# Norms of a two-layer decoder step on one core: a third staging tile, the second group's norm steps in front of the splitting of weights, and a last norm with its factors in PSUM

## The chip, the core and the metric

The kernel runs on one core of one Trainium2 chip. The metric is the device time of one execution in microseconds. The profiled execution has a span of 1143.7 us, from its first to its last instruction, and a mean granted TensorE clock of 0.989 (1.00 is 2.4 GHz, a level at half of it is 1.2 GHz).

## What is computed

One inference step of a decoder with two layers, in f32, for 512 new prompt tokens and 8 sample tokens, 1024 features. Each layer has a mixer (attention over a sliding window in the first, gated linear attention, GLA, in the second) and a gated ConvFFN, and behind each of these four sublayers stands a layer norm. The change is in the norms.

```python
def layer_norm(x, g, b):
    mu = jnp.mean(x, -1, keepdims=True)
    var = jnp.mean(jnp.square(x - mu), -1, keepdims=True)
    return (x - mu) * lax.rsqrt(var + LN_EPS) * g + b

for i in range(DEPTH):                                   # DEPTH = 2
    m = swa(x, ...) if i % 2 == 0 else gla(x, ...)       # with w_qkv / w_gla, w_mix_o
    x = layer_norm(ALPHA * x + m, ln_mix_g[i], ln_mix_b[i])
    f = conv_ffn(x, ...)        # gelu(causal_conv3(x @ w_gate)) * (x @ w_value) @ w_down
    x = layer_norm(ALPHA * x + f, ln_ffn_g[i], ln_ffn_b[i])
```

## The kernel before, in words

**Data.** Features lie on the partitions: `x` is 8 tiles of 128 features by the tokens. The 520 tokens form two groups, a (256) and b (264). To keep f32 accuracy each operand of a product is split into a high part and a low part (`wh`, `wl` of a weight; `xh`, `xl` of x; for group a both parts lie in `xs_a`, for b they are `xh_b`, `xl_b`), and a product is three matmuls: `wh`·`xh` (L193), `wh`·`xl` (L195), `wl`·`xh` (L196).

**Units.** A unit is 128 output features of one weight, which for a group takes 8 x 3 matmuls into one PSUM bank `accp`. The units follow each other through the phases: attention's q, k, v (10), its output projection (8), the first FFN (three parts, each of `w_up` units and 8 `w_down` units), GLA, its output projection, and the second FFN. Group a runs 4 or 5 units ahead of b (`LEADS`), so that a's norm can run while b's last products fill TensorE, and b's norm while a's first products of the next phase do.

**Weights.** `load_unit` issues a 512 KB load on SP's queue into a staging tile `raw` (`RAWS` of them, 2), ScalarE copies the high part (`wh`, L165) and VectorE subtracts it for the low part (`wl`, L168). A staging tile is free again when its `wl` is done. There are `WSLOTS` = 6 slots for split weights, and one more pool for an extra unit at the start of an FFN. I call the units of the phase behind a norm e, e+1, and so on. At three of the four norms the weights of e+1 to e+5 are "late": they are split in `parts` (L177, L179), held by `issue_after` behind instructions of a's norm. The extra unit is e+6, split at L165 and L168.

**The norm.** `ln_chunk` runs behind each output unit: it adds the product to x (L243 or L245), squares it on ScalarE (L263) and adds to the running sums (L275, L276; most of b's on GpSimd, the last ones on VectorE). `ln_end` multiplies the sums by ones on TensorE (L283 and L285, into the PSUM banks `tp` and `pv`), copies the mean (L288) and its square (L289) on ScalarE, subtracts the mean from six of the eight x tiles on GpSimd (L291) and from two on VectorE (L299), forms minus the variance `nv` (L292), takes its logarithm and an exponential on ScalarE (L300, L301), improves that by one Newton step on VectorE (L302, L303, L305) and has the factor in `pv`. Then for each of the 8 tiles VectorE scales (L321), ScalarE writes the high part (L322) and VectorE the low part (L323). ScalarE's first Gelu of the new phase (L620) needs another table, and TensorE's first matmul of b in the new phase needs `xh_b`.

**The last norm** writes no high and low parts. VectorE scales pairs of tiles (L311), ScalarE (L314) or VectorE (L316) applies gain and bias, and SP stores each pair of y (L317).

**What sets the order.** The program is written unit by unit. Generators that `yield n` are resumed n slots later (`spawn`, `due`), and each engine's final order is chosen by a scheduler at build time from the dependences and its own time line.

Of the kernel before, what the change touches and what calls it, by code (L numbers as in the profile page):

```python
# [95 lines left out]
class Net:  # L96
# [74 lines left out]
    def parts(self, u, h, l, r):  # L171


        norm = self.norm if self.norm and self.slot < self.norm[0] else None
        behind = lambda ins: self.tc.issue_after(ins) if norm else ExitStack()
        with behind(norm and norm[1]):
# [57 lines left out]
    def ln_chunk(self, g, m, ps, scaled, last=False):
# [41 lines left out]
        (nc.gpsimd if m < p2 else nc.vector).tensor_tensor(g.s2, g.s2, q, op=ALU.add)  # L276

    def ln_end(self, g, i, last=False):
# [23 lines left out]
        nc.vector.tensor_tensor(q, r, r, op=ALU.mult)  # L302
        nc.vector.scalar_tensor_tensor(q, q, 0.5, nv, op0=ALU.mult, op1=ALU.mult)  # L303
        rp = r if last else e2
        nc.vector.scalar_tensor_tensor(rp, q, 1.5, r, op0=ALU.add, op1=ALU.mult)  # L305
# [834 lines left out]
```

## Time and profile before

| | |
|---|---|
| median of 3 runs | 1143.75 us (1142.8 to 1144.4) |
| profiled execution | 1145.38 us, span 1143.7 us |
| TensorE (PE) busy | 1105.9 us, 97% of the span, 8806 matmuls |
| VectorE (DVE) busy | 784.1 us, 69% |
| ScalarE (ACT) busy | 566.9 us, 50% |
| GpSimd (POOL) busy | 321.8 us, 28% |
| DMA | 122.81 MB, 107 GB/s over the span |

TensorE is busy for nearly all of the span, so the places to look at are the few in which it is not, and what ended each of these waits. Times within the program are us from the span's start.

### The profile page before, as it was taken

How to read it: one execution, taken by the hardware profiler on the slowest of the kernel's cores; microseconds unless marked ns; L12 is line 12 of the kernel's file. 1: busy time of each engine (PE TensorE's matmuls, PEld its weight loads, DVE VectorE, ACT ScalarE, POOL GpSimd, SP SyncE). 2: the span in 40 equal slices, each digit the busy share in tenths (PEclk: the TensorE clock that was granted, in tenths of full speed). 3: DMA queues.
4: the chain of work that ended last, by engine and by line, in shares of the span. 5: the costliest groups of instructions: out<-in, count | busy, mean ns of one | idle time of the engine just before them, and what ended most of it. 6: DMA issues, size and time to landing. Idle time of an engine off the chain costs nothing.

```text
span 1143.7 us, 22908 instructions
## 1 busy us (share of the span) xinstructions
PE 1105.9 (97%) x8806; PEld 1056.7 (92%) x8806; DVE 784.1 (69%) x1628; ACT 566.9 (50%) x1251; POOL 321.8 (28%) x589
## 2 busy tenths in 40 slices
PE   8999998999999999999899999998999999999995
PEld 7997798999999999999899999898999999999994
DVE  8897578755665566568867877788755665566657
ACT  5677555534553245435545655455524553245433
POOL 4575584400110001255311100383400110011344
PEclk9999999999999999999899999999999999999998
DMA  7453022333323223242125355332333232232222
GB/s 239 150 178 93 16 75 93 111 93 119 103 93 109 94 95 109 75 132 96 56 87 162 114 176 173 118 101 92 111 98 125 93 109 95 93 112 93 75 64 75
DMA packets 53788, 122.81 MB, mean 107 GB/s; under 512 B 6792, under 2 KB 27312, under 8 KB 53680
## 3 DMA queue, kind: packets, MB, share of 16 engines
q1 hardware_dynamic: 51664, 119.61, 32.7%
q10 hardware_dynamic: 2016, 1.75, 0.5%
q8 instruction: 69, 1.13, 0.4%
q14 instruction: 39, 0.32, 0.1%
HBM read 108.67 MB, written 8.47 MB: 102 GB/s over the span
## 4 chain that ended last, share of the span: by engine, by line
PE 74%; DVE 12%; DMA 5%; ACT 3%; issue 2%; POOL 2%; SPq 0%; ACTq 0%; DVEq 0%; POOLq 0%
PE accp L214 15%; PE accp L195 15%; PE accp L193 15%; PE accp L196 15%; PE accp L215 8%; DMA vb<-dv 3%; DVE wl L168 1%; DVE xs_a L323 1%; DVE wl L179 1%; DMA raw<-in_w_up 1%; DVE sgla L877 1%; DMA raw<-in_w_qkv 1%; DVE x_a L321 1%; DMA qs<-hl 1%; PE pv L521 1%
## 5 line engine op out<-in xcount | busy, mean ns | idle before, releaser
L168 DVE TENSOR_TENSOR wl<-raw,wh 128x1024 fp32r<-128x1024 f32 (+2 forms) x174 | 210.5, 1212 | 110.5 <-ACT wh L165 109.9
L165 ACT ACTIVATE wh<-raw 128x1024 fp32r<-128x1024 f32 (+2 forms) x170 | 175.9, 1035 | 208.3 <-PE accp L195 187.2
L193 PE MATMUL accp<-xh_b,wh 128*128 128x264 f32 x976 | 271.7, 278 | 7.4 <-ACT xh_b L322 7.4
L195 PE MATMUL accp<-xl_b,wh 128*128 128x264 f32 x976 | 270.6, 278 | 0.0
L196 PE MATMUL accp<-xh_b,wl 128*128 128x264 f32 x976 | 270.5, 277 | 0.0
L214 PE MATMUL accp<-xs_a,wh 128*128 128x512 f32 x576 | 196.3, 382 | 0.0
L193 PEld LDWEIGHTS accp<-xh_b,wh 128*128 128x128 f32 x976 | 185.0, 190 | 8.3 <-ACT xh_b L322 7.8
L195 PEld LDWEIGHTS accp<-xl_b,wh 128*128 128x128 f32 x976 | 184.6, 189 | 2.5 <-issue 0.4
L196 PEld LDWEIGHTS accp<-xh_b,wl 128*128 128x128 f32 x976 | 184.4, 189 | 0.8 <-issue 0.6
L215 PE MATMUL accp<-xs_a,wl 128*128 128x256 f32 x576 | 145.4, 273 | 0.0
L193 PE MATMUL accp<-hh_b,wh 128*128 128x264 f32 x480 | 134.0, 279 | 1.7 <-ACT hh_b L221 1.2
L195 PE MATMUL accp<-hl_b,wh 128*128 128x264 f32 x480 | 134.4, 280 | 0.3 <-DVE hl_b L561 0.2
L196 PE MATMUL accp<-hh_b,wl 128*128 128x264 f32 x480 | 133.6, 278 | 0.0
L214 PEld LDWEIGHTS accp<-xs_a,wh 128*128 128x128 f32 x576 | 109.1, 189 | 11.4
L193 PE MATMUL accp<-xs_a,wh 128*128 128x256 f32 x400 | 113.6, 286 | 0.9 <-ACT wh L165 0.9
L196 PE MATMUL accp<-xs_a,wl 128*128 128x256 f32 x400 | 112.6, 284 | 1.4 <-DVE wl L168 0.8
L215 PEld LDWEIGHTS accp<-xs_a,wl 128*128 128x128 f32 x576 | 110.2, 191 | 1.9
L195 PE MATMUL accp<-xs_a,wh 128*128 128x256 f32 x384 | 109.0, 284 | 0.6 <-DVE xs_a L222 0.3
L193 PEld LDWEIGHTS accp<-hh_b,wh 128*128 128x128 f32 x480 | 91.5, 191 | 2.4 <-ACT hh_b L221 1.6
L195 PEld LDWEIGHTS accp<-hl_b,wh 128*128 128x128 f32 x480 | 91.3, 190 | 1.8 <-DVE hl_b L561 0.4
L196 PEld LDWEIGHTS accp<-hh_b,wl 128*128 128x128 f32 x480 | 91.4, 190 | 0.2
L225 POOL COPY hist<-aext 128x2 f32<-128x2 f32 x44 | 10.7, 244 | 276.8 <-DVE aext L608 274.0
(327 smaller groups left out, 2500.5 us busy)
## 6 DMA issues: line engine op xcount, KB each, us to landing
raw<-in_w_up SPq DMA_DIRECT2D x88, 512.0 KB, 3.4
raw<-in_w_down SPq DMA_DIRECT2D x32, 512.0 KB, 3.4
raw<-in_w_gla SPq DMA_DIRECT2D x24, 512.0 KB, 3.4
raw<-in_w_mix_o SPq DMA_DIRECT2D x16, 512.0 KB, 4.1
raw<-in_w_down SPq DMA_DIRECT2D x16, 384.0 KB, 3.0
qs<-hl SPq DMA_DIRECT2D x64, 64.0 KB, 2.1
sgla<-in_state_gla SPq DMA_DIRECT2D x16, 256.0 KB, 2.8
vb<-dv SPq DMA_DIRECT2D x16, 256.0 KB, 3.7
```

Source lines behind the costliest of these rows:

```text
L165: nc.scalar.activation(h[:, c], r[:, c], AF.Copy)
L168: nc.vector.tensor_tensor(l[:, c], r[:, c], h[:, c].bitcast(F32), op=ALU.subtract)
L179: self.nc.vector.tensor_tensor(l, r, h.bitcast(F32), op=ALU.subtract)
L193: nc.tensor.matmul(o, h[:, ks], xh, start=k == 0, stop=False)
L195: nc.tensor.matmul(o, h[:, ks], xl, start=False, stop=False)
L196: nc.tensor.matmul(o, l[:, ks], xh, start=False, stop=not tail and k == nt - 1)
L214: both = lambda: nc.tensor.matmul(o, h[:, ks], in_turn(rs[:, k].rearrange("p t q j -> p t (q j)")), start=k == 0, stop=last)
L215: low = lambda: nc.tensor.matmul(o[:, :P], l[:, ks], in_turn(rh[:, k]), start=False, stop=False)
L321: v = nc.vector.scalar_tensor_tensor(x[:, m], x[:, m], sc(m), rp, op0=ALU.mult, op1=ALU.mult)
L323: xl = nc.vector.scalar_tensor_tensor(g.xl[:, m], parted(x[:, m]), bi(m), g.xh[:, m].bitcast(F32), op0=ALU.add, op1=ALU.subtract)
L521: mm = nc.tensor.matmul(pv[64 * v:64 * v + 64, b * P:(b + 1) * P], self.vtok[:, kb, 64 * v:64 * v + 64], parts[v][w][:, b], start=i == 0, ...
L877: late(nc.vector.scalar_tensor_tensor(s[:, j], vb[:, j], kraw[:, b:b + 1], s[:, j], op0=ALU.mult, op1=ALU.add))
```

## The change

Five edits, in the diff below.

- `RAWS` is 3: a load may start when the third last unit's low part is done.
- `parts` takes a place j instead of the norm's state and holds the two splits behind marked instructions: the first late unit (j = 1) behind a's exponential and a's scales, j = 2 behind a's low parts, j = 3 and 4 behind b's sums, and j = 5 (unit e+5) and j = 6 (the extra unit, which is late too now) behind b's exponential and b's factor.
- Group a's 8 scales come first, and its 8 low parts 3 slots later in a piece, behind b's latest addition to x. Group b's low parts come behind all its scales too.
- Two tiles of the norm share others' room (`sb` takes `nv`'s, `sa` takes `r`'s).
- In the last norm `nv`, the Newton step and the factor are in PSUM, VectorE subtracts the mean from four tiles (from PSUM) and GpSimd from four, and each pair's scale is held behind the affine step of VectorE on the pair before, with ScalarE on tiles 0, 1, 2, 4, 6 and VectorE on 3, 5, 7.

```diff
-RAWS = 2
+RAWS = 3
...
             if late:
-                self.spawn(self.parts(u, h[:, c], l[:, c], r[:, c]), 1)
+                self.spawn(self.parts(late, h[:, c], l[:, c], r[:, c]), (0, 1, 2, 2, 2, 1, 0)[late])
...
+    def parts(self, j, h, l, r):
+        for _ in range(3):
+            yield 0
+        behind = lambda what: self.tc.issue_after(self.marks[what]) if what in self.marks else ExitStack()
+        with behind({1: "exp_a", 3: "high_a", 5: "exp_b", 6: "exp_b"}.get(j)):
             self.nc.scalar.activation(h, r, AF.Copy)
-        with behind(norm and norm[2 if u == norm[4] else 3]):
+        with behind({1: "rows_a", 2: "low_a", 3: "sums_b", 4: "sums_b", 5: "factor_b", 6: "factor_b"}[j]):
             self.nc.vector.tensor_tensor(l, r, h.bitcast(F32), op=ALU.subtract)
...
+        if last:
+            nv, vr = self.mtile("sc")[:, :n], self.mtile("sc")[:, :n]
-        for m in range(2, KD) if last else range(NSUB):
+        for m in range(2, NSUB) if last else range(NSUB):
             nc.gpsimd.tensor_tensor(x[:, m], x[:, m], mu, op=ALU.subtract)
...
             if last:
-                nc.vector.tensor_tensor(x[:, 0:2], x[:, 0:2], mu.unsqueeze(1).broadcast_to([P, 2, n]), op=ALU.subtract)
+                for xp in (x[:, 0:2], x[:, NSUB:KD]):
+                    nc.vector.tensor_tensor(xp, xp, e1.unsqueeze(1).broadcast_to([P, 2, n]), op=ALU.subtract)
...
+        if last:
+            nc.vector.tensor_tensor(vr, nv, r, op=ALU.mult)
+            q = nv
+            nc.vector.scalar_tensor_tensor(q, vr, 0.5, r, op0=ALU.mult, op1=ALU.mult)
+        else:
+            nc.vector.tensor_tensor(q, r, r, op=ALU.mult)
+            nc.vector.scalar_tensor_tensor(q, q, 0.5, nv, op0=ALU.mult, op1=ALU.mult)
+        rp = e2
+        factor = nc.vector.scalar_tensor_tensor(rp, q, 1.5, r, op0=ALU.add, op1=ALU.mult)
...
+                with self.tc.issue_after(behind) if behind else ExitStack():
+                    nc.vector.tensor_tensor(xp, xp, rp.unsqueeze(1).broadcast_to([P, 2, n]), op=ALU.mult)
                 for j in (m, m + 1):
-                    if j in (0, 2, 4, 5, 7):
+                    if j in (0, 1, 2, 4, 6):
                         nc.scalar.activation(x[:, j], x[:, j], AF.Identity, scale=sc(j), bias=bi(j))
                     else:
-                        nc.vector.tensor_scalar(x[:, j], x[:, j], sc(j), bi(j), op0=ALU.mult, op1=ALU.add)
+                        behind = nc.vector.tensor_scalar(x[:, j], x[:, j], sc(j), bi(j), op0=ALU.mult, op1=ALU.add).ins
...
         for m in range(KD):
             v = nc.vector.scalar_tensor_tensor(x[:, m], x[:, m], sc(m), rp, op0=ALU.mult, op1=ALU.mult)
+            xh = nc.scalar.activation(g.xh[:, m], parted(x[:, m]), AF.Identity, bias=bi(m))
+        self.marks.update({"rows_" + g.name: v.ins, "high_" + g.name: xh.ins})
         if g.i == 0:
+            yield 3
+            yield 0
+        with ExitStack() if g.i else self.tc.issue_after(self.marks["add_b"]):
+            for m in range(KD):
+                xl = nc.vector.scalar_tensor_tensor(g.xl[:, m], parted(x[:, m]), bi(m), g.xh[:, m].bitcast(F32), op0=ALU.add, op1=ALU.subtract)
...
-            late = not extra and self.units[u][1] and any(e - 5 <= done < e for e in (...))
+            e = min((p for p in self.phases[2:4] + self.phases[5:] if p > u - WSLOTS), default=u)
+            late = late or (0 if extra else max(0, u - e))
```

The first place is VectorE's order in b's first norm (behind attention's output projection), from b's last sums on; line numbers are those of the kernel that each piece is of. Before:

```order
L275 TENSOR_TENSOR s_b<-s_b,x_b 128x264
L276 TENSOR_TENSOR s_b<-s_b,sq 128x264
L610 SCALAR_TENSOR_TENSOR conv<-aext,par,conv 128x256
L611 SCALAR_TENSOR_TENSOR conv<-aext,par,conv 128x256
L179 TENSOR_TENSOR wl<-raw,wh 128x1024 x2
L292 SCALAR_TENSOR_TENSOR nv<-msq,pv 128x264
L299 TENSOR_TENSOR x_b<-x_b,tp 128x264 x2
L610 SCALAR_TENSOR_TENSOR conv<-aext,par,conv 128x256
L302 TENSOR_TENSOR msq<-r 128x264
L611 SCALAR_TENSOR_TENSOR conv<-aext,par,conv 128x256
L632 TENSOR_TENSOR hprod<-conv,accp 128x256
L303 SCALAR_TENSOR_TENSOR msq<-msq,nv 128x264
```

Behind these rows come L168 (`wl` of the extra unit), L632, L305, L222 and the 8 scales L321. And of the change, where L271 and L272 are the sums, L178 is `wl`, L291 is `nv`, L647 multiplies behind the Gelu, L310 forms the factor and L329 scales:

```order
L271 TENSOR_TENSOR s_b<-s_b,x_b 128x264
L272 TENSOR_TENSOR s_b<-s_b,sq 128x264
L178 TENSOR_TENSOR wl<-raw,wh 128x1024 x2
L625 SCALAR_TENSOR_TENSOR conv<-aext,par,conv 128x256
L626 SCALAR_TENSOR_TENSOR conv<-aext,par,conv 128x256
L291 SCALAR_TENSOR_TENSOR nv<-msq,pv 128x264
L299 TENSOR_TENSOR x_b<-x_b,tp 128x264 x2
L307 TENSOR_TENSOR msq<-r 128x264
L647 TENSOR_TENSOR hprod<-conv,accp 128x256
L308 SCALAR_TENSOR_TENSOR msq<-msq,nv 128x264
L310 SCALAR_TENSOR_TENSOR pv<-msq,r 128x264
L178 TENSOR_TENSOR wl<-raw,wh 128x1024
```

The second convolution's two steps, one of the two products with hprod and the extra unit's `wl` (the last row) have gone behind the factor. Next come 5 scales (L329), the `wl` of unit e+5 (before the second of the two ahead of `nv`), and the other 3 scales. The two `wl` ahead of `nv` are those of e+3 and e+4 now, and one `wl` fewer stands ahead of the sums.

The second place is TensorE's order around the first matmul of b in the new phase, with buffer numbers; `wh_2404` is the weight of unit e. Before, `wh_2660` being that of unit e+5:

```order
L193 MATMUL accp_2904<-xs_a_86,wh_2660 128x256
L195 MATMUL accp_2904<-xs_a_86,wh_2660 128x256
L196 MATMUL accp_2904<-xs_a_86,wl_2661 128x256
L193 MATMUL accp_2933<-xh_b_89,wh_2404 128x264
L193 MATMUL accp_2975<-xs_a_86,wh_2737 128x256
L195 MATMUL accp_2975<-xs_a_86,wh_2737 128x256
```

And of the change, where `wh_2658` and `wl_2659` are those of unit e+5:

```order
L194 MATMUL accp_2870<-xs_a_86,wl_2615 128x256
L191 MATMUL accp_2904<-xs_a_86,wh_2658 128x256
L193 MATMUL accp_2904<-xs_a_86,wh_2658 128x256
L191 MATMUL accp_2933<-xh_b_89,wh_2404 128x264
L194 MATMUL accp_2904<-xs_a_86,wl_2659 128x256
L191 MATMUL accp_2904<-xs_a_86,wh_2658 128x256
```

Before, all 24 matmuls of a with e+5 stand in front of b's first matmul; now 2 do, and the 22 others stand behind it, the first of them with `wl_2659`. The norm before the second FFN has the same shape.

The third place is VectorE's end of the program, from b's `nv` on. Before:

```order
L292 SCALAR_TENSOR_TENSOR nv<-msq,pv 128x264
L296 TENSOR_TENSOR x_b<-x_b,mu 128x528
L302 TENSOR_TENSOR msq<-r 128x264
L303 SCALAR_TENSOR_TENSOR msq<-msq,nv 128x264
L305 SCALAR_TENSOR_TENSOR r<-msq,r 128x264
L311 TENSOR_TENSOR x_b<-x_b,r 128x528 x3
L316 TENSOR_SCALAR x_b<-x_b,par 128x264
L311 TENSOR_TENSOR x_b<-x_b,r 128x528
L316 TENSOR_SCALAR x_b<-x_b,par 128x264 x2
```

And of the change, where `tp`, `pv` and `sc` are PSUM banks:

```order
L291 SCALAR_TENSOR_TENSOR sc<-msq,pv 128x264
L296 TENSOR_TENSOR x_b<-x_b,tp 128x528 x2
L303 TENSOR_TENSOR sc<-sc,r 128x264
L305 SCALAR_TENSOR_TENSOR sc<-sc,r 128x264
L310 SCALAR_TENSOR_TENSOR pv<-sc,r 128x264
L320 TENSOR_TENSOR x_b<-x_b,pv 128x528 x2
L325 TENSOR_SCALAR x_b<-x_b,par 128x264
L320 TENSOR_TENSOR x_b<-x_b,pv 128x528
L325 TENSOR_SCALAR x_b<-x_b,par 128x264
L320 TENSOR_TENSOR x_b<-x_b,pv 128x528
L325 TENSOR_SCALAR x_b<-x_b,par 128x264
```

One instruction more subtracts the mean, each of the seven others between it and the affine steps has one operand in PSUM, and the pairs end one after the other.

## Rows read from the trace of the kernel before

**Rows 1.** Windows: stretch and length, busy us (instructions) by engine, clock, DMA share, GB/s

```profile
30.00:140.00 110.00, 104.41 (x930) 94.89 (x929) 88.39 (x269) 73.63 (x263) 65.21 (x119) 0.98 0.38 110
160.00:175.00 15.00, 14.90 (x131) 14.58 (x130) 14.85 (x26) 8.16 (x17) 9.93 (x11) 1.00 0.19 58
175.00:190.00 15.00, 11.22 (x94) 10.90 (x95) 12.74 (x23) 10.05 (x20) 7.71 (x11) 1.00 0.48 154
...
540.00:560.00 20.00, 17.30 (x109) 15.28 (x109) 18.12 (x42) 11.89 (x29) 6.07 (x6) 0.83 0.16 53
```

**Rows 2.** TensorE's waits: what waited and for what, us in total, times, longest

```profile
PE accp L193 <- ACT xh_b L322: 7.4, 2, 3.9
PE accp L704 <- ACT v_a L771: 2.5, 1, 2.5
```

**Rows 3.** Windows behind the waits of b's first and second norm, columns as in rows 1

```profile
188.00:192.00 4.00, 2.80 (x18) 2.80 (x18) 4.00 (x11) 4.00 (x10) 0.18 (x1) 0.79 0.37 131
...
552.00:556.00 4.00, 4.00 (x20) 3.71 (x20) 3.60 (x10) 0.49 (x2) 0.00 (x0) 0.56 0.00 0
```

**Rows 4.** Timeline of DVE, b's first norm: start, us, instruction, count [idle before <-releaser]

```profile
167.30 3.48 DVE L323 SCALAR_TENSOR_TENSOR xs_a<-x_a,par,xs_a 128x256 fp32r<-128x256 f32 x6
...
175.19 0.42 DVE L276 TENSOR_TENSOR s_b<-s_b,sq 128x264 f32<-128x264 f32 x1
...
179.97 1.23 DVE L179 TENSOR_TENSOR wl<-raw,wh 128x1024 fp32r<-128x1024 f32 x1 [1.44 <-ACT wh L177]
181.11 0.42 DVE L292 SCALAR_TENSOR_TENSOR nv<-msq,pv 128x264 f32<-128x264 f32 x1
181.45 0.76 DVE L299 TENSOR_TENSOR x_b<-x_b,tp 128x264 f32<-128x264 f32 x2
...
185.41 1.76 DVE L168 TENSOR_TENSOR wl<-raw,wh 128x1024 fp32r<-128x1024 f32 x1
...
187.43 0.43 DVE L305 SCALAR_TENSOR_TENSOR pv<-msq,r 128x264 f32<-128x264 f32 x1
...
188.10 3.28 DVE L321 SCALAR_TENSOR_TENSOR x_b<-x_b,par,pv 128x264 f32<-128x264 f32 x8
```

**Rows 5.** Timeline of ACT in the same stretch

```profile
178.88 1.06 ACT L177 ACTIVATE wh<-raw 128x1024 fp32r<-128x1024 f32 x1 [1.61 <-DMA raw<-in_w_up]
179.84 0.36 ACT L288 COPY mu<-tp 128x264 f32<-128x264 f32 x1
...
182.46 1.28 ACT L620 ACT_TABLE_LOAD   x1
...
188.62 3.63 ACT L322 ACTIVATE xh_b<-x_b,par 128x264 fp32r<-128x264 f32 x8
```

**Rows 6.** Timeline of POOL, b's first and last norm

```profile
180.28 5.81 POOL L291 TENSOR_TENSOR x_b<-x_b,mu 128x264 f32<-128x264 f32 x6 [3.54 <-ACT mu L288]
...
1130.70 5.74 POOL L291 TENSOR_TENSOR x_b<-x_b,mu 128x264 f32<-128x264 f32 x6 [7.47 <-ACT mu L288]
```

**Rows 7.** Timeline of DVE, b's last norm

```profile
1128.91 0.42 DVE L243 TENSOR_TENSOR x_b<-x_b,accp 128x264 f32<-128x264 f32 x1
...
1132.33 0.57 DVE L302 TENSOR_TENSOR msq<-r 128x264 f32<-128x264 f32 x1 [0.32 <-ACT r L301]
...
1133.82 0.86 DVE L305 SCALAR_TENSOR_TENSOR r<-msq,r 128x264 f32<-128x264 f32 x1
1134.71 2.91 DVE L311 TENSOR_TENSOR x_b<-x_b,r 128x528 f32<-128x528 f32 x3
...
1138.50 0.73 DVE L316 TENSOR_SCALAR x_b<-x_b,par 128x264 f32<-128x264 f32 x2
```

**Rows 8.** Timeline of PE, the last matmul of the last product

```profile
1128.04 0.28 PE L196 MATMUL accp<-hh_b,wl 128*128 128x264 f32 x1
```

**Rows 9.** Timeline of SP's queue, the last stores

```profile
1138.02 2.24 SPq L317 DMA_DIRECT2D out_y<-x_b  x4
```

**Rows 10.** Timeline of PE at the start, TensorE's last wait for a weight there

```profile
24.47 0.38 PE L193 MATMUL accp<-xs_a,wh 128*128 128x256 f32 x1 [0.38 <-ACT wh L165]
```

More of the change, by code (lines that the diff above doesn't have):

```diff
@@ L56 @@
 LATEB = 14
-HOLD = 5
 WIDE = 4
@@ L169, in load_unit @@
         self.w[u] = (h, l)
[L171 to L176, printed above, removed]
+    def parts(self, j, h, l, r):
[3 more added lines that the diff above has]
+        with behind({1: "exp_a", 3: "high_a", 5: "exp_b", 6: "exp_b"}.get(j)):
             self.nc.scalar.activation(h, r, AF.Copy)
-        with behind(norm and norm[2 if u == norm[4] else 3]):
+        with behind({1: "rows_a", 2: "low_a", 3: "sums_b", 4: "sums_b", 5: "factor_b", 6: "factor_b"}[j]):
             self.nc.vector.tensor_tensor(l, r, h.bitcast(F32), op=ALU.subtract)
-        yield from ()
     def product(self, g, u, rh, rl):
@@ L228, in mtile @@
         return self.mps.tile([P, 512], F32, name=tag, bufs=2 if tag == "sc" else 1)
-    def next_phase(self):
-        return min(p for p in self.phases if p > self.unit)
     def ln_chunk(self, g, m, ps, scaled, last=False):
@@ L242, in ln_chunk @@
         if scaled:
-            nc.vector.tensor_tensor(x[:, m], x[:, m], ps, op=ALU.add)
+            add = nc.vector.tensor_tensor(x[:, m], x[:, m], ps, op=ALU.add)
         else:
-            nc.vector.scalar_tensor_tensor(x[:, m], x[:, m], ALPHA, ps, op0=ALU.mult, op1=ALU.add)
+            add = nc.vector.scalar_tensor_tensor(x[:, m], x[:, m], ALPHA, ps, op0=ALU.mult, op1=ALU.add)
+        self.marks["add_" + g.name] = add.ins
         if m == 0:
@@ L253, in ln_chunk @@
             if not scaled:
-                sa = c("sa")
+                sa = c("r")
                 nc.scalar.activation(sa, mp, AF.Copy, scale=KD / ALPHA)
@@ L301, in ln_end @@
         self.exp = nc.scalar.activation(r, r, AF.Exp, scale=-0.5).ins
[L302 to L305, printed above, removed]
+        if last:
[7 more added lines that the diff above has]
+        factor = nc.vector.scalar_tensor_tensor(rp, q, 1.5, r, op0=ALU.add, op1=ALU.mult)
+        self.marks.update({"exp_" + g.name: self.exp, "factor_" + g.name: factor.ins})
         sc = lambda m: self.par[:, C_LNG + i * KD + m:C_LNG + i * KD + m + 1]
@@ L321, in ln_end @@
             v = nc.vector.scalar_tensor_tensor(x[:, m], x[:, m], sc(m), rp, op0=ALU.mult, op1=ALU.mult)
-            nc.scalar.activation(g.xh[:, m], parted(x[:, m]), AF.Identity, bias=bi(m))
-            xl = nc.vector.scalar_tensor_tensor(g.xl[:, m], parted(x[:, m]), bi(m), g.xh[:, m].bitcast(F32), op0=ALU.add, op1=ALU.subtract)
+            xh = nc.scalar.activation(g.xh[:, m], parted(x[:, m]), AF.Identity, bias=bi(m))
+        self.marks.update({"rows_" + g.name: v.ins, "high_" + g.name: xh.ins})
         if g.i == 0:
-            self.norm = self.slot + HOLD, self.exp, v.ins, xl.ins, self.next_phase() + 1
+            yield 3
[3 more added lines that the diff above has]
+                xl = nc.vector.scalar_tensor_tensor(g.xl[:, m], parted(x[:, m]), bi(m), g.xh[:, m].bitcast(F32), op0=ALU.add, op1=ALU.subtract)
+        self.marks["low_" + g.name] = xl.ins
         for m in range(KD):
@@ L982, in more, with next_unit @@
         return self.nu < end - XEND
-    def next_unit(self, extra):
+    def next_unit(self, extra, late=0):
         u = self.nu
@@ L987, in next_unit @@
             self.nu += 1
-            done = u - WSLOTS
-            late = not extra and self.units[u][1] and any(e - 5 <= done < e for e in (*self.phases[2:3], *self.phases[3:4], *self.phases[5:6]))
+            e = min((p for p in self.phases[2:4] + self.phases[5:] if p > u - WSLOTS), default=u)
+            late = late or (0 if extra else max(0, u - e))
             self.load_unit(u, extra=extra, late=late)
@@ L998, in run @@
         self.attn_open()
-        self.later, self.slot, self.seq, self.norm = [], 0, 0, None
+        self.later, self.slot, self.seq, self.marks = [], 0, 0, {}
         for i, u in self.order():
@@ L1002, in run @@
             _, _, f, a, pre = self.units[u]
-            if i == 1:
-                self.unit = u
             if i == 0 and pre:
```

8 lines of the change are left out of this document (4 added, 4 removed).

## The prediction

> **What bounds the kernel now.** I read the windows first. In 160 to 175 us TensorE is busy for 14.90 of 15 us with 131 matmuls, one in 0.114 us, and that is how most of the program looks [rows 1]. A change to the norms can therefore only win where TensorE stands. The windows show three such places outside the two ends: 5.6 us spread over attention (30 to 140), 3.8 us in 175 to 190 and 2.7 us in 540 to 560, there with the clock at 0.83 [rows 1]. The third norm has the shape of the first. Then the waits: TensorE waits twice for `xh_b`, 7.4 us in total, the longer 3.9, at the norms ahead of the two FFNs, and once for 2.5 us at the norm ahead of GLA [rows 2]. That last one is put down to `v_a`, but what the matmul at L704 reads is `xh_b`, which ScalarE writes there after it. Each wait costs more than its length: in the 4 us behind the first the granted clock is 0.79, in 552 to 556 it is 0.56 [rows 3], which is nearly all of that stretch at 1.2 GHz.
>
> Now back from the wait, in the timelines of the first norm. `xh_b` begins at 188.62 [rows 5], just behind the first of the scales at 188.10, which had to wait for the factor (L305) at 187.43, and ahead of that stood a 1.76 us `wl` [rows 4]. The chain begins with `nv` at 181.11. The sums were issued at 175.19, so 5.9 us lie between the sums and `nv`. In them VectorE's `wl` stood 1.44 us for ScalarE's `wh` [rows 4], which itself stood 1.61 us for a load, and ScalarE's copy of the mean was queued behind that `wh` [rows 5]. So a late load delays the norm. This is what the third staging tile and the new order act on.
>
> The end is the other place: the last product's last matmul starts at 1128.04 [rows 8], and the last stores are issued from 1138.02 on for 2.24 us [rows 9]. All 10 us between are the last norm, with nothing beside it.
>
> **First norm of b, step by step.** *Up to `nv`.* One `wl` of about 1.2 us fewer stands ahead of the sums on VectorE, which had no idle time there, so the sums end near 174.4 in place of 175.6. The three tiles let the loads of e+3 and e+4 start one unit sooner, by more than the 1.61 us of the wait, so I cost that wait at nothing now. Then come two `wl` (1.2 each, up to 1.76 beside GpSimd [rows 4]) and two steps of the convolution of some 0.5: `nv` would stand between 177.9 and 179. I take 178.5, 2.6 us earlier, for GpSimd's six subtractions (5.81 us [rows 6]) now begin with the earlier mean and lie beside these `wl`.
>
> *From `nv` to `xh_b`.* Before, ScalarE's table load starts 1.35 us behind `nv` (182.46 [rows 5]) and takes 1.28; the Gelu behind it takes some 0.4. In the new order the product with hprod needs this Gelu and stands ahead of the last two factor steps, so three steps of about 0.4 (as L305 [rows 4]) end at 1.35 + 1.28 + 0.4 + 1.2 = 4.3 behind `nv`. The extra unit's `wl` (1.2), the first scale (3.28/8 = 0.41 [rows 4]) and its high part (3.63/8 = 0.45 [rows 5]) follow: the first `xh_b` is ready 6.35 us behind `nv`, at 184.9. Before it was ready at 189.1. That is 4.2 us gained on this chain.
>
> *What is late next.* TensorE doesn't cash it in. Its order puts b's first matmul 22 matmuls sooner, behind only two of unit e+5, so it arrives 22 x 0.114 = 2.5 us earlier, at about 183. And the next matmul in its queue reads `wl` of e+5, which VectorE does behind the five scales: 4.3 + 1.2 + 5 x 0.41 + 1.2 = 8.75 behind `nv`, 187.3. The whole of a's unit e+5 is queued behind this matmul, and b's next ones behind that. The 22 matmuls that before lay ahead of the wait bring TensorE at 187.3 + 2.5 = 189.8 to where it was at 189.1: +0.7. With `nv` at 177.9 it is +0.1. The 8 low parts of a, in a piece behind b's additions now, make TensorE wait for some of a's tail products (0.58 each [rows 4], as GpSimd works beside them), but this only uses up time that it would stand at 183 anyway. I take +0.3 for this norm and the same for the third. The low clock behind the wait stays.
>
> **Second norm.** There is no Gelu and no table between `nv` and the factor: 1.35 + 3 steps of 0.4 + 1.2 + 0.41 + 0.45, so `xh_b` stands about 4.6 behind a `nv` that comes 2.6 earlier, where in the first norm before it was 8.0. The 2.5 us wait [rows 2] goes. With the clock, (1 - 0.83) x 20 = 3.4 us at stake in this window [rows 1], up to 5.9 us could be won. But VectorE now does b's scales (3.28) and half of b's low parts (4 x 0.41) ahead of the scan of GLA's decay, 4.9 us, and a's q and k and the state's products wait for that. So a second wait, on the decay, takes the place of part of the first. Between 0 and -5.9 I take -2.7, just short of half.
>
> **Last norm.** Factors: L302, L303 and L305 take from 1132.33 to the first pair at 1134.71, 2.4 us, at up to 0.86 each with two SBUF operands beside GpSimd's subtractions [rows 6, 7]. With one operand in PSUM the same shape takes 0.38 to 0.43 though GpSimd works (L299 at 181.45 [rows 4]). The two subtractions of the mean that VectorE now makes take 1.4 and end 0.35 after the exponential, so 2.4 becomes 0.35 + 1.1: -0.9. Pairs: 2.91/3 = 0.97 each, the last affine step ends at 1139.23 [rows 7], 4.5 us behind the first pair's start; now four of about 0.70 and three affine steps of 0.36, then 0.25 of ScalarE's last step: 4.1, -0.4. The mean: b's last addition starts 0.6 behind the last matmul's end [rows 7, 8], because VectorE is busy with a's last norm, which gets shorter by the same means: -0.5. Stores: the four are issued in 2.24 us in a row [rows 9]; spread out, the last finds the queue free: -0.3. Sum -2.1, between 0 (transfers decide) and -3.
>
> The Trainium skill's page "VectorE: DVE Perf Modes", section "Rules for kernel authors", speaks against this part: for elementwise work on a matmul's output it wants either the 1x rate accepted or the data copied from PSUM to SBUF first where many operations follow, and the change goes the other way. By that rule factors and pairs win nothing and the tail would give -0.8, the whole -3.3. The trace differs in this stretch: 0.38 from PSUM against 0.86 from SBUF alone.
>
> **Start and scheduler.** The third tile lets a load of the start begin sooner: TensorE's 0.38 us wait [rows 10] goes, -0.4. What the scheduler shuffles elsewhere, in attention above all, I cost at 0; the cover there is TensorE's queue, and without it no more than the 5.6 us idle in 30 to 140 [rows 1] can be won or half as much lost; I let it count for 1.5 either way.
>
> **Sum.** -0.4 + 0.3 - 2.7 + 0.3 - 2.1 = -4.6. The profiled execution took 1145.38 and would take 1140.8; the median of the three runs is 1.6 lower, 1143.75, and gives 1139.2.
>
> **Rivals.**
> - *The steps in front do cure the waits.* If VectorE's queue drains so that `wl` of e+5 is ready by 183, the 7.4 us [rows 2] go, and some 0.8 of low clock behind each [rows 3]: 9 us more, 1130; half of it 1135. For it: `nv` loses its wait on the load. Against: two `wl`, five scales and the Gelu stand in a row on VectorE. Chance 0.20.
> - *Only the end gains.* The decay's wait gives all of the second norm back: 1143.75 - 2.1 + 0.2 = 1141.8. For it: the 4.9 us put ahead of the scan. Chance 0.13.
> - *It does nothing.* The transfers of y set the end, or pairs wait for GpSimd, and norms trade wait for wait: 1143.5. Against: 0.97 a pair lies on the path, plain to see. Chance 0.09.
> - *Slower.* `wl` of e+5 behind the five scales decides. If `nv` is not earlier (the third tile is taken by the extra unit's load, so the load of e+4 is as late as before), it is ready at 181.1 + 8.75 = 189.9, TensorE is 22 matmuls further at 192.4, 3.3 later than before, twice: with -0.4 and -2.1 that is +4.1, 1147.9. With the second norm at 0 it decides, against the bound below, from 2.4 us a norm, `nv` less than 0.9 us earlier. Chance 0.13.
>
> **Numbers.** My forecast has 0.45. A measurement of this kernel tells about 0.2% (2.3 us) from no change. Faster takes my forecast, the first rival and a part of the second, 0.73; same 0.14; slower 0.13. The range goes from 1131.5, which leaves out the full cure, to 1143.8, which leaves out the slower case; the forecast's own range is 1136.5 to 1141.5.
>
> **What would show it.** Right: TensorE's wait for `xh_b` L322 falls below 3 us and one for `wl` L178 of 2 us or more appears at both FFN norms; `nv` of b's first norm near 178.5; the factor steps and pairs at 0.35 to 0.43 and 0.6 to 0.7; the last store issued 2 us earlier behind the last matmul. Wrong: no wait for `wl` there (first rival), or a clock of 1.00 through 540 to 560, or `nv` near 181.

## The result, and the profile after

The changed kernel takes 1149.63 us (median of 6 runs, 1148.17 to 1151.91) where the kernel before takes 1144.08 (6 runs): a ratio of 1.0044, with a 95% interval of 1.0029 to 1.0058, or 5 us. I had forecast 1139.2, faster. The profiled execution took 1151.91, the longest of the six, with a span of 1150.2 and a clock of 0.984.

The windows of the changed kernel, columns as in [rows 1]:

```profile
30.00:140.00 110.00, 104.26 (x930) 95.62 (x929) 88.84 (x270) 73.16 (x262) 67.78 (x121) 0.98 0.38 111
...
175.00:190.00 15.00, 11.02 (x85) 10.32 (x84) 13.89 (x24) 10.63 (x23) 6.58 (x10) 0.92 0.47 144
...
540.00:560.00 20.00, 16.59 (x114) 14.76 (x113) 16.40 (x36) 9.57 (x21) 5.05 (x6) 0.90 0.33 106
```

Attention is as it was. At the first norm TensorE starts 85 matmuls in place of 94. The last window can't be compared as it stands: TensorE comes to it 2.9 us later than before, and its low clock goes on behind 560 (0.63 in 560 to 564). What can be compared is the time between two like instructions. Each norm has a product of a's sums with the ones (L283 before, L279 now), and its starts divide the program into stages; first of the kernel before, then of the changed one:

```profile
156.61 0.59 PE L283 MATMUL tp<-s_a,ones_a 128*128 128x256 f32 x2
...
517.57 0.59 PE L283 MATMUL tp<-s_a,ones_a 128*128 128x256 f32 x2
...
753.94 0.70 PE L283 MATMUL tp<-s_a,ones_a 128*128 128x256 f32 x2
...
1115.63 0.59 PE L283 MATMUL tp<-s_a,ones_a 128*128 128x256 f32 x2
```

```profile
157.67 0.59 PE L279 MATMUL tp<-s_a,ones_a 128*128 128x256 f32 x2
...
520.50 0.59 PE L279 MATMUL tp<-s_a,ones_a 128*128 128x256 f32 x2
...
760.63 0.59 PE L279 MATMUL tp<-s_a,ones_a 128*128 128x256 f32 x2
...
1124.23 0.59 PE L279 MATMUL tp<-s_a,ones_a 128*128 128x256 f32 x2
```

| stage, up to the next product of a's sums | forecast | before, us | changed, us | difference |
|---|---|---|---|---|
| start and attention | -0.4 | 156.6 | 157.7 | +1.1 |
| first norm of b, first FFN | +0.3 | 361.0 | 362.8 | +1.9 |
| second norm, GLA and its projection | -2.7 | 236.4 | 240.1 | +3.8 |
| third norm, second FFN | +0.3 | 361.7 | 363.6 | +1.9 |
| last norm, up to the end | -2.1 | 28.0 | 26.0 | -2.1 |
| the whole span | -4.6 | 1143.7 | 1150.2 | +6.5 |

The profiled executions are 6.5 us apart, the medians 5.5. Only the last norm did what was forecast; the largest miss is at the norm ahead of GLA. TensorE's waits, which answer to [rows 2]:

```profile
PE accp L194 <- DVE wl L178: 3.6, 2, 1.8
PE accp L191 <- ACT wh L176: 2.7, 2, 1.5
PE accp L191 <- ACT wh L163: 2.4, 2, 1.4
PE accp L191 <- ACT xh_b L330: 2.0, 2, 1.0
```

The wait for `xh_b` has fallen from 7.4 to 2.0 us, as expected. What stands in its place is a wait for both parts of a weight: L176 and L178 split the late units, and the two waits of each are at the two FFN norms. L163 is the split of an ordinary unit; its longer wait, 1.4 us, is at the norm ahead of GLA. TensorE's timeline at the first norm shows the others in a row; the first three matmuls here are all that it issues between 183.98, when it last had work, and 188.82:

```profile
185.18 0.38 PE L191 MATMUL accp<-xs_a,wh 128*128 128x256 f32 x1 [1.20 <-ACT wh L176]
185.39 0.28 PE L193 MATMUL accp<-xs_a,wh 128*128 128x256 f32 x1
186.65 0.38 PE L191 MATMUL accp<-xh_b,wh 128*128 128x264 f32 x1 [0.98 <-ACT xh_b L330]
188.82 0.58 PE L194 MATMUL accp<-xs_a,wl 128*128 128x256 f32 x1 [1.79 <-DVE wl L178]
```

Before, one wait of 3.5 us stood there, up to b's first matmul at 189.20. VectorE's timeline, which answers to [rows 4]:

```profile
167.90 5.22 DVE L338 SCALAR_TENSOR_TENSOR xs_a<-x_a,par,xs_a 128x256 fp32r<-128x256 f32 x8
...
175.21 0.44 DVE L272 TENSOR_TENSOR s_b<-s_b,sq 128x264 f32<-128x264 f32 x1
...
180.18 0.42 DVE L291 SCALAR_TENSOR_TENSOR nv<-msq,pv 128x264 f32<-128x264 f32 x1
...
184.42 1.22 DVE L178 TENSOR_TENSOR wl<-raw,wh 128x1024 fp32r<-128x1024 f32 x1
185.55 2.08 DVE L329 SCALAR_TENSOR_TENSOR x_b<-x_b,par,pv 128x264 f32<-128x264 f32 x5
187.55 1.22 DVE L178 TENSOR_TENSOR wl<-raw,wh 128x1024 fp32r<-128x1024 f32 x1
```

From the sums to `nv` are 5.0 us in place of 5.9, and from `nv` to the second `wl`'s end 8.6; that last one is unit e+5's, on which TensorE stands. Counted from the product of a's sums, `nv` comes after 22.5 us where before it took 24.5. And ScalarE's timeline, which answers to [rows 5]:

```profile
181.52 1.28 ACT L635 ACT_TABLE_LOAD   x1
...
183.14 1.99 ACT L176 ACTIVATE wh<-raw 128x1024 fp32r<-128x1024 f32 x2
...
186.07 2.23 ACT L330 ACTIVATE xh_b<-x_b,par 128x264 fp32r<-128x264 f32 x5
```

The second of these two `wh` is that of e+5. It ends at 185.1 and lets TensorE's matmul at 185.18 go: held behind b's exponential, it comes behind the table load, the Gelu and the extra unit's `wh`. The clock behind these waits, first of the changed kernel (answers to [rows 3]), then of the kernel before in the same stretches:

```profile
186.00:190.00 4.00, 1.56 (x6) 1.36 (x7) 4.00 (x10) 3.81 (x10) 0.20 (x1) 0.68 0.49 141
190.00:194.00 4.00, 4.00 (x21) 4.00 (x20) 4.00 (x11) 0.60 (x2) 0.00 (x0) 0.50 0.31 121
```

```profile
186.00:190.00 4.00, 0.80 (x7) 0.80 (x8) 4.00 (x9) 2.46 (x7) 1.58 (x4) 1.00 0.36 128
190.00:194.00 4.00, 4.00 (x24) 4.00 (x23) 4.00 (x11) 2.25 (x6) 0.00 (x0) 0.57 0.01 3
```

In these 8 us (1 - 0.68) x 4 + (1 - 0.50) x 4 = 3.3 us of full clock are missing, in place of 1.7. Part of that falls on time in which TensorE stood anyway. What it costs is seen in the matmuls: 23 follow each other by 0.21 us and not by 0.11 (189.20 to 194.10 in TensorE's timeline), where before 15 did (190.50 to 193.70), so some 2.3 us are lost in place of 1.5. The third norm looks the same. The end, in contrast, did what was forecast. The last matmul, the factor and the pairs, and the stores, which answer to [rows 7 to 9]:

```profile
1136.64 0.28 PE L194 MATMUL accp<-hh_b,wl 128*128 128x264 f32 x1
```

```profile
1141.57 0.44 DVE L310 SCALAR_TENSOR_TENSOR pv<-sc,r 128x264 f32<-128x264 f32 x1
1142.04 1.32 DVE L320 TENSOR_TENSOR x_b<-x_b,pv 128x528 f32<-128x528 f32 x2
...
1145.53 0.42 DVE L325 TENSOR_SCALAR x_b<-x_b,par 128x264 f32<-128x264 f32 x1
```

```profile
1143.91 2.62 SPq L326 DMA_DIRECT2D out_y<-x_b  x4
```

From the last matmul's start to the span's end are 1150.2 - 1136.6 = 13.6 us; before, 1143.7 - 1128.0 = 15.7. So the end gives 2.1 us back, and some 8.6 are lost ahead of it.

### The profile page after: what moved, and what is told of

It reads as the page before. It is cut to its first block, busy times and chain, and to the rows that moved or that the text cites. A ratio compares the mean times of both kernels' runs of the same rounds, so it can differ in the third digit from the quotient of the medians.

```text
span 1150.2 us, 22921 instructions
## 1 busy us (share of the span) xinstructions
PE 1111.7 (97%) x8806; PEld 1062.9 (92%) x8806; DVE 781.9 (68%) x1630; ACT 565.2 (49%) x1251; POOL 312.0 (27%) x585
## 4 chain that ended last, share of the span: by engine, by line
PE 74%; DVE 12%; ACT 4%; DMA 3%; issue 3%; POOL 3%; SPq 1%; DVEq 0%; POOLq 0%; ACTq 0%
PE accp L194 15%; PE accp L212 15%; PE accp L193 15%; PE accp L191 15%; PE accp L213 8%; DMA vb<-dv 2%; DVE wl L178 1%; DMA raw<-in_w_qkv 1%; DVE wl L166 1%; DVE xs_a L338 1%; DVE de L907 1%; ACT wh L163 1%; PE pv L536 1%; DVE x_b L329 1%; DVE sgla L892 1%
## 5 line engine op out<-in xcount | busy, mean ns | idle before, releaser
L166 DVE TENSOR_TENSOR wl<-raw,wh 128x1024 fp32r<-128x1024 f32 (+2 forms) x172 | 205.6, 1196 | 106.1 <-ACT wh L163 105.5
L163 ACT ACTIVATE wh<-raw 128x1024 fp32r<-128x1024 f32 (+2 forms) x168 | 173.6, 1034 | 197.5 <-PE accp L193 194.4
L213 PE MATMUL accp<-xs_a,wl 128*128 128x256 f32 x576 | 145.4, 273 | 0.0
L191 PE MATMUL accp<-xs_a,wh 128*128 128x256 f32 x400 | 115.9, 292 | 5.5 <-ACT wh L176 2.7
L194 PE MATMUL accp<-xs_a,wl 128*128 128x256 f32 x400 | 115.7, 291 | 5.1 <-DVE wl L178 3.6
L193 PE MATMUL accp<-xs_a,wh 128*128 128x256 f32 x384 | 112.2, 293 | 0.3 <-DVE xs_a L220 0.3
```

Source lines behind the costliest of these rows:

```text
L163: nc.scalar.activation(h[:, c], r[:, c], AF.Copy)
L166: nc.vector.tensor_tensor(l[:, c], r[:, c], h[:, c].bitcast(F32), op=ALU.subtract)
L191: nc.tensor.matmul(o, h[:, ks], xh, start=k == 0, stop=False)
L193: nc.tensor.matmul(o, h[:, ks], xl, start=False, stop=False)
L194: nc.tensor.matmul(o, l[:, ks], xh, start=False, stop=not tail and k == nt - 1)
L213: low = lambda: nc.tensor.matmul(o[:, :P], l[:, ks], in_turn(rh[:, k]), start=False, stop=False)
```

## The experiments

Two theories stood against each other. The order theory: the loss is made where the splitting of weights was put behind b's steps. The tile theory: it comes from the third staging tile and what the scheduler rearranges for it. Ratios are to the kernel before, run beside each on the same chip.

| kernel | median us | ratio, 95% interval |
|---|---|---|
| last norm alone | 1141.93 | 0.9973 (0.9962 to 0.9983) |
| third tile alone | 1137.69 | 0.9937 (0.9916 to 0.9958) |
| change without the last norm | 1153.47 | 1.0069 (1.0052 to 1.0087) |
| change, e+5 in front | 1144.49 | 0.9991 (0.9978 to 1.0005) |
| third tile and last norm | 1135.74 | 0.9911 (0.9897 to 0.9926) |
| e+5 in front, extra unit free | 1141.73 | 0.9964 (0.9948 to 0.9979) |
| change, a's low parts back | 1152.76 | 1.0064 (1.0047 to 1.0081) |
| e+5 in front, extra free, low parts back | 1141.40 | 0.9966 (0.9951 to 0.9982) |
| the last one, old holds ahead of GLA | 1132.00 | 0.9879 (0.9865 to 0.9894) |
| change, low parts back, old holds ahead of GLA | 1141.51 | 0.9969 (0.9955 to 0.9983) |
| third tile and last norm, factors in SBUF | 1139.39 | 0.9943 (0.9927 to 0.9958) |

**The last norm alone**, on the kernel before.

```diff
+            nv, vr = self.mtile("sc")[:, :n], self.mtile("sc")[:, :n]
-        for m in range(2, KD) if last else range(NSUB):
+        for m in range(2, NSUB) if last else range(NSUB):
...
-        rp = r if last else e2
+        rp = e2
...
+                with self.tc.issue_after(behind) if behind else ExitStack():
...
```

> The kernel before with the last norm's edits alone (factors in PSUM, four tiles each for GpSimd and VectorE, pairs one after the other). Order theory (the loss is made at the three earlier norms, where the low and high parts of unit e+5 were put behind b's factor and exponential) and tile theory (the loss comes from the third staging tile and what the scheduler rearranges for it) expect the same here: some 2 us less than before, since the stretch from the last matmul to the end took about 2 us less in the changed kernel. No change or slower would mean that the last norm has a part in the loss.

3.1 us less (2 to 4.4). From the last matmul at 1125.90 to the span's end at 1139.1 are 13.2 us. The last norm has no part in the loss.

**The third tile alone.**

```diff
-RAWS = 2
+RAWS = 3
...
-            sb = c("sb")
+            sb = c("nv")
...
-                sa = c("sa")
+                sa = c("r")
```

> The kernel before with three staging tiles and the two shared norm tiles, all else as before. Order theory: no loss, 0 to 3 us less than before, since the loads come sooner and the norm's order of steps is the old one; TensorE's wait for xh_b at the two FFN norms is 2 to 3.9 us. Tile theory: at least 2 us more than before, made in attention, GLA and at the norms.

7.2 us less (5 to 10), more than either theory had. The tile theory falls. TensorE's wait for `xh_b` and the windows behind the two FFN norms:

```profile
PE accp L193 <- ACT xh_b L322: 4.1, 2, 2.4
```

```profile
188.00:192.00 4.00, 3.83 (x34) 3.64 (x34) 4.00 (x11) 2.73 (x6) 0.00 (x0) 1.00 0.00 0
...
782.00:786.00 4.00, 4.00 (x38) 4.00 (x37) 4.00 (x12) 2.98 (x7) 0.00 (x0) 1.00 0.01 4
```

The two waits have shrunk by 3.3 us in total [rows 2], and behind them the clock stays at its upper level in this execution, where before it was 0.79 behind the first [rows 3]. Here a shorter wait paid twice.

**The change without the last norm**, the changed kernel with the old `if last` branch of `ln_end`.

```diff
-            nv, vr = self.mtile("sc")[:, :n], self.mtile("sc")[:, :n]
...
-        rp = e2
+        rp = r if last else e2
...
```

> The changed kernel with the last norm of before. Both theories: some 2 us more than the changed kernel, 7 us more than before. If it equals the changed kernel, the last norm's edits do nothing there.

1.0069 against 1.0044, 2.9 us more than the changed kernel, as expected: the two parts add up.

**Unit e+5 in front.**

```diff
-        with behind({1: "exp_a", 3: "high_a", 5: "exp_b", 6: "exp_b"}.get(j)):
+        with behind({1: "exp_a", 3: "high_a", 5: "high_a", 6: "exp_b"}.get(j)):
...
-        with behind({..., 4: "sums_b", 5: "factor_b", 6: "factor_b"}[j]):
+        with behind({..., 4: "sums_b", 5: "sums_b", 6: "factor_b"}[j]):
```

> The changed kernel with unit e+5's high part held behind a's high parts and its low part behind b's sums, as unit e+4's are; the extra unit stays behind b's factor. Order theory: TensorE's waits for wh and wl L176/L178 at the FFN norms go (3.6 + 2.7 us in the changed kernel), only the one for xh_b stays, and the clock is low for 3.4 us there and not for 6.8: 4 to 6 us less than the changed kernel, 1143.5 to 1145.5. Tile theory: at most 1 us less than the changed kernel.

6 us less than the changed kernel, as the order theory had it (0.9991 against 1.0044). No wait for L176 or L178 is among TensorE's seven longest, and `xh_b` is back at 3.7 us. But third tile and last norm should then give 10 us over the kernel before, so 9 are still lost elsewhere.

**Third tile and last norm**, the first two edits together.

```diff
-RAWS = 2
+RAWS = 3
...
+            nv, vr = self.mtile("sc")[:, :n], self.mtile("sc")[:, :n]
...
```

> The kernel before with three staging tiles and the last norm's edits, the three earlier norms in their old order. If the parts add up, 0.9937 x 0.9973 = 0.991 of the time before, 10 us less, some 1135 us where before takes 1145, and the new order of steps at the three norms is then worth about +15 us. If the third tile's gain and the last norm's share a cause, 1138 us.

0.9911, the product of the two. So the new order at the norms is worth 1.0044 - 0.9911, +15 us.

**The extra unit free**, on top of e+5 in front.

```diff
-                        self.next_unit(True, WSLOTS)
+                        self.next_unit(True)
```

> The last kernel of the first four (unit e+5's split in front, as e+4's) with the extra unit not held behind b's exponential and factor, as before the change. If the splits behind b's factor are what costs, b's scales come 1.2 us sooner behind the factor at both FFN norms: 2 to 4 us less than 1144.5, 1140.5 to 1142.5. If the piece of a's low parts and what it delays is what is left, no more than 1 us less.

3.1 us less than with the hold (0.9964 against 0.9991), within the expected 2 to 4.

**a's low parts back**, on the changed kernel.

```diff
             xh = nc.scalar.activation(g.xh[:, m], parted(x[:, m]), AF.Identity, bias=bi(m))
+            xl = nc.vector.scalar_tensor_tensor(g.xl[:, m], ...)
-        if g.i == 0:
-            yield 3
-            yield 0
-        with ExitStack() if g.i else self.tc.issue_after(self.marks["add_b"]):
...
```

> The changed kernel with a's low parts issued with a's scales again, as before, all holds of the weights' parts kept. If the holds cost nearly all, the same as the changed kernel within 1.5 us (TensorE's waits for xs_a low parts, 1.6 us in total, stood ahead of other waits). If the low parts' move has its own share, 3 us less or more.

Not faster: 1.0064 against 1.0044, intervals that overlap. The edit issues b's low parts with its scales again too, but at b's first norm they stay behind all 8 of them in VectorE's order. A gain of the 3 us that the rival had is ruled out: the low parts' move is not a cause that these runs can tell.

**All three**: e+5 in front, extra unit free, low parts back.

> Both edits on top of the kernel with unit e+5 in front: extra unit free, a's low parts back. What is left of the new order is e+3, e+4 and e+5 behind b's sums. If these holds are harmless by themselves, this comes to the kernel with only the third tile and the last norm, about 1135; if b's sums in front (which puts a's decay behind b's scales at the norm ahead of GLA) cost something by themselves, it stays 2 us or more above that.

0.9966, the same as without the low parts' edit. 6 us are left over third tile and last norm, and they come with the rest of the new order, e+3 to e+5 behind b's sums above all.

**Old holds ahead of GLA**, on top of that: at this one norm the late units' splits are held behind a's exponential, scales and low parts, as before, and the splits are written into the program where they stood before.

```diff
-                self.spawn(self.parts(late, h[:, c], l[:, c], r[:, c]), (0, 1, 2, 2, 2, 1, 0)[late])
+                self.spawn(self.parts(late, h[:, c], l[:, c], r[:, c], self.old), 1 if self.old else (0, 1, 2, 2, 2, 1, 0)[late])
...
-        for _ in range(3):
+        for _ in range(0 if old else 3):
...
-        with behind({...}.get(j)):
+        with behind("exp_a" if old else {...}.get(j)):
...
-        with behind({...}[j]):
+        with behind(("rows_a" if j == 1 else "low_a") if old else {...}[j]):
...
+            self.old = e == self.phases[3]
```

> The last kernel (extra unit free, a's low parts back, e+5 in front) with the holds of before at the norm ahead of GLA, so that only the two FFN norms keep e+3 to e+5 behind b's sums. If the 5.7 us between that kernel and the one with the tile and the last norm alone are made at the norm ahead of GLA, where b's scales and low parts stand ahead of the decay, this takes 1134 to 1136.5 us and TensorE's waits for wh and wl behind the rank's product go. If they are made at the FFN norms, 1139 us or more.

1132.0 us, 0.9879 (0.9865 to 0.9894): faster than the kernel before by 13.8 us and than any other kernel here. The new order at the norm ahead of GLA costs 10 us (0.9966 - 0.9879), more than the 6 that were left. The new order at the two FFN norms, without the two holds behind b's factor, is a gain of 3.7 us over tile and last norm alone (0.9911 - 0.9879). TensorE at the norm ahead of GLA, first with the new holds there (all three), then with the old ones:

```profile
542.52 1.27 PE L712 MATMUL accp<-xh_b,wh 128*128 128x264 f32 x8 [1.57 <-ACT v_a L779]
...
545.11 1.59 PE L712 MATMUL accp<-xl_b,wh 128*128 128x264 f32 x4 [0.60 <-DVE xl_b L331]
548.13 0.58 PE L191 MATMUL accp<-xs_a,wh 128*128 128x256 f32 x1 [1.42 <-ACT wh L163]
...
549.39 0.58 PE L194 MATMUL accp<-xs_a,wl 128*128 128x256 f32 x1 [0.46 <-DVE wl L166]
```

```profile
543.90 1.88 PE L712 MATMUL accp<-xh_b,wh 128*128 128x264 f32 x4 [2.40 <-ACT v_a L779]
545.57 1.06 PE L770 MATMUL sc<-q_a,k_a 128*128 128x128 f32 x4
```

With the old holds there is one wait, and behind it stand a's products of GLA, ready. With the new ones b comes 1.4 us sooner (0.6 of it were won ahead of this norm), but nothing of a is ready behind it, and four waits come in a row. VectorE's timeline says why, in the same order:

```profile
538.83 2.09 DVE L329 SCALAR_TENSOR_TENSOR x_b<-x_b,par,pv 128x264 f32<-128x264 f32 x5
...
543.99 0.68 DVE L730 TENSOR_TENSOR_SCAN dcum<-reset,dmn 128x256 f32<-128x256 f32 x1
...
549.25 0.42 DVE L755 SCALAR_TENSOR_TENSOR q_a<-accp,ep 128x256 f32<-128x256 f32 x1
```

```profile
538.11 1.12 DVE L730 TENSOR_TENSOR_SCAN dcum<-reset,dmn 128x256 f32<-128x256 f32 x1
...
542.54 2.09 DVE L329 SCALAR_TENSOR_TENSOR x_b<-x_b,par,pv 128x264 f32<-128x264 f32 x5
544.54 0.42 DVE L755 SCALAR_TENSOR_TENSOR q_a<-accp,ep 128x256 f32<-128x256 f32 x1
```

The scan of a's decay comes 5.9 us later and a's q 4.7 us later, because b's scales and four of its low parts now stand ahead. The windows, in the same order, show 97 matmuls at a clock of 0.83 against 120 at 0.91:

```profile
540.00:560.00 20.00, 15.87 (x97) 13.99 (x96) 12.50 (x31) 9.18 (x21) 0.42 (x1) 0.83 0.09 26
```

```profile
540.00:560.00 20.00, 17.59 (x120) 15.64 (x119) 18.25 (x48) 12.38 (x32) 2.44 (x5) 0.91 0.11 32
```

**The changed kernel with old holds ahead of GLA** (and a's low parts back), all holds kept at the FFN norms.

```diff
+        with behind("exp_a" if old else {1: "exp_a", 3: "high_a", 5: "exp_b", 6: "exp_b"}.get(j)):
```

> The changed kernel with a's low parts back (1152.8 us) and the holds of before at the norm ahead of GLA; the FFN norms keep all the holds of the change. Norm ahead of GLA as the place: about 5 to 6 us less, 1147. FFN norms as the place of nearly all: 1150 us or more.

0.9969 against 1.0064: 11 us less, twice what was expected. The kernel here and the one before it differ by the two holds behind b's factor at the FFN norms: 0.9969 - 0.9879, 10 us over both.

The products of a's sums divide these kernels too. Each stage of the profiled execution against the same stage of the kernel before, in us:

| kernel | start, attention | first norm | norm ahead of GLA | third norm | last norm |
|---|---|---|---|---|---|
| changed kernel | +1.1 | +1.9 | +3.8 | +1.9 | -2.1 |
| third tile and last norm | -1.2 | -2.7 | -1.7 | -1.3 | -2.0 |
| change, a's low parts back | -1.4 | +2.0 | +4.6 | +4.1 | -2.0 |
| the same, old holds ahead of GLA | +0.2 | 0.0 | -1.4 | +0.3 | -2.0 |
| e+5 in front, extra free, low parts back | -1.6 | -3.7 | +3.6 | -1.8 | -2.0 |
| the same, old holds ahead of GLA | -0.9 | -3.8 | -2.6 | -4.1 | -2.0 |

In both pairs that differ by the holds ahead of GLA alone, the new ones cost 6 us in that norm's stage (5.9 and 6.1), as was expected. The rest of the 10 and 11 us stands at stages that this edit doesn't touch, the third norm's above all (3.8 and 2.3); the runs don't show why. The two holds behind b's factor cost 3.8 us at the first norm and 4.4 at the third. Each row is one execution, and the first column, which no hold touches, goes from -1.6 to +1.1: a single difference of that size proves nothing.

**The last norm in SBUF**, on tile and last norm: the split of tiles and the order of the pairs stay.

```diff
-            nv, vr = self.mtile("sc")[:, :n], self.mtile("sc")[:, :n]
...
-        rp = e2
+        rp = r if last else e2
...
-    nc.vector.tensor_tensor(xp, xp, e1.unsqueeze(1).broadcast_to([P, 2, n]), op=ALU.subtract)
+    nc.vector.tensor_tensor(xp, xp, mu.unsqueeze(1).broadcast_to([P, 2, n]), op=ALU.subtract)
```

> The kernel with the tile and the last norm, but with the last norm's nv, Newton step, factor and mean in SBUF; the split of tiles, the order of the pairs and the stores stay. If PSUM makes the steps short, the factor steps beside GpSimd take up to 0.9 us in place of 0.43 and the tail grows by 0.7 to 1.2 us, 1136.5. If the new split and order alone do it, the same tail of 13.6 us from the last matmul's start.

0.9943 against 0.9911, 3.7 us more; the two intervals lie next to each other. In the profile the stretch from the last matmul's start (1118.63) to the end (1134.3) is 15.7 us, that of the old last norm, against 13.6 (1121.2 to 1134.8) in PSUM. VectorE's factor steps and GpSimd's four subtractions, first in SBUF, then in PSUM:

```profile
1123.74 0.97 DVE L303 TENSOR_TENSOR msq<-r 128x264 f32<-128x264 f32 x1
1124.74 0.85 DVE L304 SCALAR_TENSOR_TENSOR msq<-msq,nv 128x264 f32<-128x264 f32 x1
...
1121.35 3.96 POOL L291 TENSOR_TENSOR x_b<-x_b,mu 128x264 f32<-128x264 f32 x4 [9.26 <-ACT mu L288]
```

```profile
1125.19 0.43 DVE L307 TENSOR_TENSOR sc<-sc,r 128x264 f32<-128x264 f32 x1
1125.65 0.44 DVE L309 SCALAR_TENSOR_TENSOR sc<-sc,r 128x264 f32<-128x264 f32 x1
...
1123.36 2.84 POOL L294 TENSOR_TENSOR x_b<-x_b,mu 128x264 f32<-128x264 f32 x4 [9.78 <-ACT mu L291]
```

PSUM makes the factor steps short, and GpSimd's too (0.99 each against 0.71). The pairs owe it nothing: they take 0.67 to 0.70 from SBUF as well, behind GpSimd's last subtraction. Split and order without PSUM win 0.8 us from the first pair to the end (8.2 for 9.0) and lose as much ahead of it (7.5 for 6.7).

## Why the prediction was wrong

**The norm ahead of GLA failed most: -2.7 was written, +3.8 us came.** The first wait did shrink as forecast: b's first matmul there stood 2.5 us before and stands 0.5 now. I had seen that a's decay would wait behind b's scales and low parts and priced this as giving back half of what the first wait's end wins. The price was that of one queue. What it left out is TensorE's side: with the old holds a's products of the recurrence lie behind b's first matmuls and fill the time until the next weights are split; without them TensorE goes straight on to a weight whose `wh` is queued on ScalarE behind the copy of the product that feeds b's decay (`z_b`), which itself waits for TensorE, and whose `wl` follows. One wait became four: 0.5, 0.6, 1.4 and 0.8 us in the changed kernel. In time the order at this norm costs 10 to 11 us against the old holds, 6 of them in its own stage.

**The FFN norms: +0.3 each was written, +1.9 us each came.** The chain behind `nv` was right: the first `xh_b` is done 6.3 us behind it for 6.35, `wl` of e+5 8.6 for 8.75. `nv` itself came 2.0 us sooner behind a's sums for the 2.6 that I took: b's sums ended 1.0 sooner for 1.2, and from there the two `wl` and the two steps of the convolution, beside GpSimd's subtractions, took 4.5 us for 4.1. In the trace's own time it is 180.18 for 181.11, because the program came 1.1 us later to this norm. The 8 low parts of a are not the reason: with them back, `nv` stands 22.6 us behind a's sums, and 22.5 with them in a piece. Two steps of the sum failed, at both norms alike. TensorE goes on at 188.82, 31.2 us behind a's sums, with 22 matmuls of e+5 still to do, which take 2.5; before it went on after 32.6 with none of them left. That is +1.0, where I had worked out +0.7 and then took +0.3 because the low parts would only use up time. And I wrote that the low clock behind the wait stays: it lasts longer, and costs 2.3 us for 1.5. I also had e+5's `wl` alone, not its `wh`, which the same hold put behind the table load. That wait lengthens nothing by itself, since `wl` ends 3.6 us later; whether it is what keeps the clock low for longer, the runs don't tell. What they do show is that the two holds behind b's factor, which make these waits, cost 10 us in time over both norms.

**The start: -0.4 was written, +1.1 us came.** The wait at 24.47 [rows 10] is gone. But the one for a `wh` ahead of it is 0.93 us (at 17.85) where before it was 0.48 (at 17.29), and the clock in 20 to 24 us is 0.57 where before it was 1.00. Third tile and last norm has 1.00 there, so the low clock is not shown to be the third tile's.

The Trainium skill's page "TensorE: Matmul & The Clock Gate", section "HAM oscillation — how this bites in real kernels", says that a kernel whose matmuls pause for data again and again runs part of its work with the clock throttled, a penalty on top of the wait. The windows above agree: 0.50 in 190 to 194 of the changed kernel, 1.00 behind the shorter waits of the third tile alone.

**The third tile: I costed it at the load's wait and -0.4 at the start.** The mechanism, a late load ahead of the norm's mean, was right. Alone it is worth 7.2 us, more than I had: in its profiled run the shorter waits at the FFN norms did not drop the clock. With the last norm's edit it gives 10 us (0.9911), and the new order of the steps takes 15 (1.0044).

**The last norm: -2.1 was written, and 2.1 us came** from the last matmul to the end, by the steps named: factors at 0.44, pairs at 0.66, b's last addition 0.3 behind the last matmul in place of 0.9. Alone it gives 3.1 us in time. The Trainium skill's page "VectorE: DVE Perf Modes", section "Rules for kernel authors", which I weighed against this part, wants the 1x rate accepted or the data copied from PSUM to SBUF first where many operations follow. Here the version with the factors in SBUF is longer by 2.1 us in the profile, so with GpSimd beside it the measurement decides for PSUM in the factor steps. The shorter pairs are not PSUM's: they begin when GpSimd is done, and take 0.67 to 0.70 from SBUF too.

**The rivals.** The slower case came nearest, 1147.9 at a chance of 0.13. It named the right instruction, `wl` of e+5 behind five scales, but its sum is another: it has 3.3 us at each FFN norm, where 1.9 came, and nothing at the norm ahead of GLA, where 3.8 came, and its condition, `nv` no earlier, was not met. So its number is near by luck. The first rival priced the low clock behind a wait at 0.8 us from a window that ends at 192; it goes on to 193.7 and costs 1.5. The scheduler's shuffle in attention, costed at 0, was 0: TensorE is busy for 104.26 us in 30 to 140, and for 104.41 before [rows 1].

## What to carry to other kernels

A step that is moved ahead delays what it passes, so price it at the engine that in the end stands: list what this engine would do in the meantime, and whether each of those is still ready. On TensorE price a wait with the clock behind it. To find where a bundle loses, divide the program by an instruction that both kernels have. When a change bundles edits, time each one alone: here one edit was worth -7 us, one -3, and the new order with its table of holds +15, and with the order put right (old holds ahead of GLA, e+5 in front, extra unit free, low parts back) the same bundle takes 0.9879 of the time before in place of 1.0044.
